# Attention scores as three fp32r products on split operands, and a scheduling priority for background work, in a decoder trunk on one core

## The chip, the cores and the metric

The kernel runs on one core of a Trainium2 chip. The metric is the device time in microseconds (us) of one execution. Five engines work side by side, each through its own instructions in order: TensorE (PE in the profile; its weight loads are listed apart as PEld), VectorE (DVE), ScalarE (ACT), GpSimd (POOL) and SyncE (SP), which issues most of the transfers. They wait for each other through semaphores.

## What is computed

One layer of a hybrid decoder trunk, for 256 positions of 2048 channels, in fp32:

```python
h = rms_norm(x, pre_g)
proj = h @ w_in        # a_u, a_v, a_g, b_x, b_g, x_q, x_g of 1024 columns each, gate_logits of 3 x 2048
y_a = spatial_gating(a_u, a_v, ...) * silu(a_g)      # layer norm of a_v over its 1024 channels first
y_b = s5_branch(b_x, ...) * silu(b_g)                # state-space scan, gelu, GLU
y_x = memory_cross_attention(x_q, rms_norm(mem, mem_g), xa_wk, xa_wv) * silu(x_g)
branch = einsum('bsnc,ncd->bsnd', stack([y_a, y_b, y_x]), w_branch)
merged = sum(sigmoid(gate_logits) * branch)
return x + rms_norm(merged @ w_out, post_g)

def memory_cross_attention(q, mem_n, w_k, w_v):      # 4 heads of 256 channels, 256 memory tokens
    k, v = mem_n @ w_k, mem_n @ w_v
    scores = einsum('bshd,bmhd->bhsm', qh, k) * 256 ** -0.5
    p = softmax(scores)
    return einsum('bhsm,bmhd->bshd', p, v)
```

## The kernel before

**Split weights.** Nearly every product is taken in the type fp32r, in three parts. `split` copies an operand to a high part in that type on ACT (L92) and subtracts it from the original on DVE, which gives the low part (L93, a buffer `hl` of 1024 columns of each; four such buffers rotate). A product is then high x high + high x low + low x high. A weight tile `raw` of 1 MB holds two such halves. A half of a block (`cm_block`, L174, L175, L177) or of a quarter (`tm_quarter`, L180 to L182) is what PE works through between two calls of `pump`; it is called a half-block below. The activations are split once and stay in SBUF.

**Stages.** The products run in this order: `w_bx`, the queries `w_xq`, the keys `wk`, the values `wv`, the gate `w_xg` of the attention branch, its gates and branch products (`merge`), then `w_av`, `w_ag`, `w_au` of the gating branch and its merge, `w_bg`, the gates, GLU and products of the S5 branch, and `w_out`. `cm_pairs` fills one PSUM pair (`acc`, two buffers in rotation) by four half-blocks and then empties it: ACT copies one part of it, and DVE adds the other (`fold_u`, L342 and L343, for queries and keys; `fold`, L230 and L231, elsewhere). PE can enter a pair only when the pair before the last one has been emptied, since it has the same bank.

**Background work.** Everything else is written as Python generators. Each call of `pump` lets every generator in the list `bg[2]` go on to its next `yield None`, and gives credit (0.47 to 1.5 a call, by the stage) to the S5 work in `bg[0]`; what a generator of `bg[2]` yields as a number is taken off that credit. In `bg[2]` are: `rms_row` (the norm of x, whose row `bc_x` is multiplied into `U` and the queries in eight steps, L330), `attn(h)` for four heads (scores L717, softmax L722 to L732, transposes `tp` L738), `attn_out(h)`, `layer_norm` (statistics L833, normalization by L371 and L374 on `H0`), and the transposes and gating steps later.

**Order.** PE's instructions stand in the order in which they are written. On DVE, ACT and the other engines a scheduler sets the order, by the place in the program and a priority; `split` of weights is written with a priority 250 places ahead (`AHEAD`), background work with none. The order is fixed when the kernel is built. The scores of a head are four products of plain fp32 operands of 128x256, each recorded as two entries in the profile (`x8`).

Of the kernel before, what the change touches and what calls it, by code (L numbers as in the profile page):

```python
# [10 lines left out]
F32R = mybir.dt.float32r  # L11
# [7 lines left out]
P = 128  # L19
# [12 lines left out]
PI2_3 = 2.0 * math.pi - PI2_1 - PI2_2  # L32
RND = 12582912.0
AHEAD = 250
BEHIND = 0
NWARM = 8
CM_OFF = 352 // 4
# [6 lines left out]
def trunk(ctx: ExitStack, tc: tile.TileContext, I, out):  # L44
    nc = tc.nc
    v, a, g, pe = nc.vector, nc.scalar, nc.gpsimd, nc.tensor
# [18 lines left out]
    def nm(s):  # L65
        n_[0] += 1
        return f"{s}_{n_[0]}"

    def slot(tag, shape, dt=F32):
        return big.tile(shape, dt, tag=tag, name=nm(tag))  # L70

    def small(shape, dt=F32):
        s = nm("sm")
        return const.tile(shape, dt, tag=s, name=s)
# [6 lines left out]
    def halves(off):  # L81
        t = hip.tile([P, 2 * 1024 + 128], F32R, tag="hl", name=nm("hl"))
        return t[:, off:off + 1024], t[:, off + 1024:off + 2048]

    def split(src, off=0):
        hi, lo = halves(off)
        with tc.high_priority(offset=AHEAD):
            split_to(hi, lo, src)
        return hi, lo

    def split_to(hi, lo, src):
        a.copy(out=hi, in_=src)  # L92
        v.tensor_tensor(out=lo, in0=src, in1=hi.bitcast(F32), op=ALU.subtract)  # L93
# [38 lines left out]
    def in_order2(z):  # L132
        return z.rearrange("p i (b c) -> p i c b", c=2)
# [29 lines left out]
    def norm_split(src, gv, dst, k0):  # L163
        for k in range(len(dst)):
            kk = k0 + k
            r = src[:, k * T:(k + 1) * T].rearrange("p (c b) -> p c b", c=2)
            hi, lo = dst[k].half(0), dst[k].half(1)
            a.activation(out=hi, in_=r, func=AF.Copy, scale=gv[:, kk:kk + 1])
            v.scalar_tensor_tensor(out=lo, in0=r, scalar=gv[:, kk:kk + 1],
                                   in1=hi.bitcast(F32), op0=ALU.mult, op1=ALU.subtract)  # L170
# [15 lines left out]
    def pump(credit):  # L186
        with tc.high_priority(offset=-BEHIND):
            pump_(credit)

    def pump_(credit):  # L190
        bg[1] += credit
        for gen in list(bg[2]):
            while True:
                c = next(gen, "end")
                if c == "end":
                    bg[2].remove(gen)
                    break
                if c is None:
                    break
                bg[1] -= c  # L200
        while bg[1] > 0:
            c = next(bg[0], "end")
            if c in (None, "end"):
                bg[1] = 0.0
                return
            bg[1] -= c
# [128 lines left out]
    def mem_half(hf):  # L335
        r = slot(f"M{hf}", [P, 2048])
        nc.sync.dma_start(out=r, in_=I["memT"][:, hf])
        with tc.high_priority(offset=AHEAD):
            norm_split(r, g_mem, mhl[hf * 8:hf * 8 + 8], hf * 8)
# [318 lines left out]
    qT = slot("X0", [P, 8, T])  # L658
# [16 lines left out]
    kT = slot("M0", [P, 8, T])  # L675
# [35 lines left out]
    def attn(h):  # L711
        for _ in range(4 * h):
            yield None
        sc = miscp.tile([P, 2, T], F32, tag="misc", name=nm("sc"))
        for qb in range(2):
            for c in range(2):
                pe.matmul(sc[:, qb, :], lhsT=qT[:, 2 * h + c, qb::2], rhs=kT[:, 2 * h + c, :],  # L717
                          start=c == 0, stop=c == 1)
        yield None
        nb = small([P, 2])  # L720
        sm = small([P, 2])
        v.tensor_reduce(out=nb, in_=sc, axis=AX.X, op=ALU.max)  # L722
        v.tensor_scalar(out=nb, in0=nb, scalar1=-1.0 / 16.0, scalar2=None, op0=ALU.mult)
        p = wk.tile([P, 2, T], F32, tag="w1", name=nm("p"))
        for qb in range(2):
            a.activation(out=p[:, qb, :], in_=sc[:, qb, :], func=AF.Exp, scale=1.0 / 16.0, bias=nb[:, qb:qb + 1],
                         accum_out=sm[:, qb:qb + 1])
        yield 0.7
        yield None
        v.reciprocal(out=sm, in_=sm)  # L730
        for qb in range(2):
            v.tensor_scalar(out=p[:, qb, :], in0=p[:, qb, :], scalar1=sm[:, qb:qb + 1], scalar2=None, op0=ALU.mult)  # L732
        yield 0.6
        yield None
        tp = miscp.tile([P, 2, T], F32, tag="misc", name=nm("tp"))
        for mb in range(2):
            for qb in range(2):
                pe.transpose(tp[:, mb, qb * P:(qb + 1) * P], p[:, qb, mb::2], ident)  # L738
        yield None
        a.copy(out=pT[:, h], in_=tp)  # L740

    def attn_out(h):
        for _ in range(h):
            yield None
        po = miscp.tile([P, 2, T], F32, tag="misc", name=nm("po"))
        for c in range(2):
            for mb in range(2):
                pe.matmul(po[:, c, :], lhsT=vv[:, mb, (2 * h + c) * P:(2 * h + c + 1) * P], rhs=pT[:, h, mb, :],  # L748
                          start=mb == 0, stop=mb == 1)
        yield None  # L750
        o = wk.tile([P, 2, T], F32, tag="w1", name=nm("o"))
        t = o.rearrange("p i (c b) -> p i c b", c=2)
        d = in_order2(sx[:, 2 * h:2 * h + 2, :])
        a.activation(out=t, in_=d, func=AF.Sigmoid)
        v.tensor_tensor(out=d, in0=po.rearrange("p i (c b) -> p i c b", c=2), in1=d, op=ALU.mult)
        yield 0.6
        v.tensor_tensor(out=t, in0=d, in1=t, op=ALU.mult)
        yield 0.6
        t = o
        d = yX[h // 2][:, 2 * (h % 2):2 * (h % 2) + 2]  # L760
        split_to(d[:, :, 0], d[:, :, 1], t)
        yield 1.2
# [3 lines left out]

    rate["cm"] = RT[2]
    bg[2].extend(attn(h) for h in range(4))
    cm_pairs(I["w_xg"], 8, xhl, evac_xg)
    bg[2].extend(attn_out(h) for h in range(4))  # L770

    mg = None
# [19 lines left out]
    def csl(c):  # L792
        return slice(c * 512, (c + 1) * 512)
# [116 lines left out]
    for bp in range(4):  # L910
# [9 lines left out]
        b = slice(2 * bp, 2 * bp + 2)  # L920
        v.tensor_tensor(out=t, in0=t, in1=u[:, b, :], op=ALU.mult)
        v.tensor_tensor(out=t, in0=t, in1=sb[:, b, :], op=ALU.mult)
        for i in range(2):
            d = yB[2 * bp + i]
# [25 lines left out]
    for c in range(4):  # L950
# [3 lines left out]
        for tb in range(2):  # L954
            d = sgB[tb][:, csl(c)]
# [68 lines left out]
    for tb in range(2):  # L1024
# [3 lines left out]
        c = slice(tb, tb + 1)  # L1028
# [107 lines left out]
```

## Time and profile before

| what | us |
|---|---|
| median of three runs (lowest, highest) | 913.08 (912.48, 913.41) |
| the profiled execution: time of its own | 913.93 |
| its span, from first to last instruction | 912.2 |
| TensorE busy | 899.3 (99%) |
| VectorE busy | 751.5 (82%) |
| ScalarE busy | 562.6 (62%) |

The mean granted clock of TensorE is 0.998 of full speed. Rows of a timeline give start, duration, engine, line, operation, tiles (written<-read) and form; "x3" stands for three instructions in a row, whose time is then that of all three. The duration of one instruction is longer than its pitch, since the next begins before it ends. Starts are counted from the span's start. A bracket gives idle time of the engine just before, and what ended it.

### The profile page before, as it was taken

How to read it: one execution, taken by the hardware profiler on the slowest of the kernel's cores; microseconds unless marked ns; L12 is line 12 of the kernel's file. 1: busy time of each engine (PE TensorE's matmuls, PEld its weight loads, DVE VectorE, ACT ScalarE, POOL GpSimd, SP SyncE). 2: the span in 40 equal slices, each digit the busy share in tenths (PEclk: the TensorE clock that was granted, in tenths of full speed). 3: DMA queues.
4: the chain of work that ended last, by engine and by line, in shares of the span. 5: the costliest groups of instructions: out<-in, count | busy, mean ns of one | idle time of the engine just before them, and what ended most of it. 6: DMA issues, size and time to landing. Idle time of an engine off the chain costs nothing.

```text
span 912.2 us, 12951 instructions
## 1 busy us (share of the span) xinstructions
PE 899.3 (99%) x4864; PEld 798.4 (88%) x4864; DVE 751.5 (82%) x1172; ACT 562.6 (62%) x962; POOL 49.8 (5%) x78
## 2 busy tenths in 40 slices
PE   8999999999999999999999999999999999999996
PEld 6999898889888888889989888889988889998896
DVE  6899967976779999899779998999889647876554
ACT  7585755855558677774456667767656546544452
POOL 1000000100001111110000010101000000000000
PEclk9999999999999999999999999999999999999999
DMA  9887665555455656665645656565655755557542
GB/s 337 312 311 294 226 231 194 202 193 191 154 205 176 242 187 227 231 212 207 231 167 186 221 203 212 190 213 203 231 190 194 258 195 203 211 185 277 194 175 93
DMA packets 32575, 195.30 MB, mean 214 GB/s; under 512 B 4224, under 2 KB 6528, under 8 KB 10752
## 3 DMA queue, kind: packets, MB, share of 16 engines
q1 hardware_dynamic: 28000, 186.08, 56.6%
q0 software_dynamic: 3936, 6.16, 3.1%
q10 hardware_dynamic: 576, 2.23, 0.6%
q8 instruction: 38, 0.62, 0.3%
q14 instruction: 25, 0.20, 0.1%
HBM read 190.39 MB, written 2.10 MB: 211 GB/s over the span
## 4 chain that ended last, share of the span: by engine, by line
PE 86%; DVE 9%; ACT 1%; DMA 1%; issue 1%; SPq 0%; DVEq 0%; ACTq 0%
PE acc L180 19%; PE acc L181 19%; PE acc L182 19%; PE acc L175 17%; PE acc L174 8%; DVE hl L93 4%; PE y L630 1%; ACT hl L92 1%; PE po L748 1%; DMA M<-memT 1%; DMA st<-start 1%; PE bu L568 1%; DVE q L374 1%; PE sc L717 1%; DVE tS L377 1%
## 5 line engine op out<-in xcount | busy, mean ns | idle before, releaser
L93 DVE TENSOR_TENSOR hl<-raw,hl 128x1024 fp32r<-128x1024 f32 x319 | 388.1, 1220 | 120.4 <-ACT hl L92 118.5
L92 ACT CAST hl<-raw 128x1024 fp32r<-128x1024 f32 x319 | 331.3, 1044 | 221.8 <-PE acc L182 139.1
L175 PE MATMUL acc<-x,hl 128*128 128x512 f32 x736 | 241.2, 382 | 0.0
L174 PE MATMUL acc<-x,hl 128*128 128x256 f32 x690 | 189.4, 274 | 2.6 <-DVE hl L93 2.6
L180 PE MATMUL acc<-hl,x 128*128 128x512 f32 x448 | 171.4, 383 | 0.0
L181 PE MATMUL acc<-hl,x 128*128 128x512 f32 x448 | 169.8, 379 | 0.0
L182 PE MATMUL acc<-hl,x 128*128 128x512 f32 x448 | 169.8, 379 | 0.0
L175 PEld LDWEIGHTS acc<-x,hl 128*128 128x128 f32 x736 | 136.8, 189 | 18.0 <-ACT hl L92 0.6
L174 PEld LDWEIGHTS acc<-x,hl 128*128 128x128 f32 x690 | 132.3, 192 | 4.5 <-DVE hl L93 3.2
L180 PEld LDWEIGHTS acc<-hl,x 128*128 128x128 f32 x448 | 84.7, 189 | 13.7 <-issue 2.5
L182 PEld LDWEIGHTS acc<-hl,x 128*128 128x128 f32 x448 | 84.7, 189 | 12.0
L181 PEld LDWEIGHTS acc<-hl,x 128*128 128x128 f32 x448 | 84.7, 189 | 11.3
L180 PE MATMUL acc<-hl,H 128*128 128x512 f32 (+1 forms) x224 | 83.6, 373 | 0.0
L181 PE MATMUL acc<-hl,H 128*128 128x512 f32 (+1 forms) x224 | 83.2, 372 | 0.0
L182 PE MATMUL acc<-hl,H 128*128 128x512 f32 (+1 forms) x224 | 83.2, 372 | 0.0
L175 PE MATMUL acc<-H,hl 128*128 128x512 f32 x192 | 62.6, 382 | 0.0
L539 POOL DMA_DIRECT2D B<-sb x30 | 25.4, 848 | 440.9 <-ACT B L534 409.4
L174 PE MATMUL acc<-H,hl 128*128 128x256 f32 x176 | 48.2, 274 | 0.2 <-DVE hl L93 0.2
L180 PEld LDWEIGHTS acc<-hl,H 128*128 128x128 f32 x224 | 42.4, 189 | 5.7 <-issue 0.4
L182 PEld LDWEIGHTS acc<-hl,H 128*128 128x128 f32 x224 | 42.4, 189 | 5.6
L181 PEld LDWEIGHTS acc<-hl,H 128*128 128x128 f32 x224 | 42.4, 189 | 5.3
L374 DVE TENSOR_TENSOR p<-bu,E 128x512 f32<-128x512 f32 x64 | 41.4, 684 | 1.7 <-PE bu L568 1.6
(256 smaller groups left out, 1217.7 us busy)
## 6 DMA issues: line engine op xcount, KB each, us to landing
raw<-w_gate SPq DMA_DIRECT2D x48, 1024.0 KB, 4.8
raw<-w_br SPq DMA_DIRECT2D x24, 1024.0 KB, 4.8
raw<-w_out SPq DMA_DIRECT2D x16, 1024.0 KB, 4.7
raw<-w_xq SPq DMA_DIRECT2D x8, 1024.0 KB, 5.2
raw<-wk SPq DMA_DIRECT2D x8, 1024.0 KB, 4.7
raw<-wv SPq DMA_DIRECT2D x8, 1024.0 KB, 4.9
raw<-w_xg SPq DMA_DIRECT2D x8, 1024.0 KB, 4.7
raw<-w_av SPq DMA_DIRECT2D x8, 1024.0 KB, 4.8
```

What stands on the lines that cost most here:

```text
L92: a.copy(out=hi, in_=src)
L93: v.tensor_tensor(out=lo, in0=src, in1=hi.bitcast(F32), op=ALU.subtract)
L174: pe.matmul(ps[:, 0:T], lhsT=wl, rhs=hl.moving(0), start=False, stop=False)
L175: pe.matmul(ps, lhsT=wh, rhs=hl.moving_both(), start=first, stop=last)
L180: pe.matmul(ps, lhsT=hl.stationary(0, tb), rhs=two(wh), start=first, stop=False)
L181: pe.matmul(ps, lhsT=hl.stationary(0, tb), rhs=two(wl), start=False, stop=False)
L182: pe.matmul(ps, lhsT=hl.stationary(1, tb), rhs=two(wh), start=False, stop=last)
L374: v.tensor_tensor(out=o, in0=i0, in1=i1, op=op)
L377: v.scalar_tensor_tensor(out=o, in0=i0, scalar=s, in1=i1, op0=o0, op1=o1)
L539: g.dma_start(out=B4[64:P].bitcast(F32), in_=rw[64:P], accum_op=ALU.add)
L568: pe.matmul(bu[:, ri, :], lhsT=B4[:, ri, :], rhs=two(U4), start=True, stop=True)
L630: pe.matmul(ps[32 * j:32 * j + 32, :], lhsT=cbt[:, cb * 4 + j, ri, :], rhs=ss[j][:, ri, :], start=ri == 0, stop=ri == 1, tile_position=(0, ...
```

## The change

Three things are written anew. The scores of a head are taken from split queries and keys: two `split_to` into a tile `qk` in the slot `H2` or `H3` (the split copies of the memory lie there until the values are done, and the attention output later), and then 12 fp32r products of 256 columns instead of four plain ones. The scores of a head come two pumps later than before, and so does `attn_out`. And all that the generators of `bg[2]` issue from `pump` gets a priority of 400 places (`URGENT`), which is ahead of the 250 of the weight splits.

```diff
+URGENT = 400
...
     def pump_(credit):
         bg[1] += credit
         for gen in list(bg[2]):
             while True:
-                c = next(gen, "end")
+                with tc.high_priority(offset=URGENT):
+                    c = next(gen, "end")
...
     def attn(h):
         for _ in range(4 * h):
             yield None
+        qk = slot(f"H{2 + h % 2}", [P, 2, 2, 2, 2, P], F32R)
+        for i, f in enumerate((qT, kT)):
+            d = f[:, 2 * h:2 * h + 2].rearrange("p k (b c) -> p k c b", c=2)
+            split_to(qk[:, i, :, :, 0], qk[:, i, :, :, 1], d)
+            yield 0.6
+        yield None
+        yield None
         sc = miscp.tile([P, 2, T], F32, tag="misc", name=nm("sc"))
         for qb in range(2):
             for c in range(2):
-                pe.matmul(sc[:, qb, :], lhsT=qT[:, 2 * h + c, qb::2], rhs=kT[:, 2 * h + c, :],
-                          start=c == 0, stop=c == 1)
+                q_, k_ = qk[:, 0, c], Pairs(qk[:, 1, c])
+                for i, (x_, y_) in enumerate(((0, 0), (0, 1), (1, 0))):
+                    pe.matmul(sc[:, qb, :], lhsT=q_[:, qb, x_], rhs=k_.moving(y_), start=c + i == 0, stop=c == 1 and i == 2)
...
     def attn_out(h):
-        for _ in range(h):
+        for _ in range(h + 2):
             yield None
```

Lines after `pump_` move by 2, those after the scores by 10: L93 is L94 in the new kernel, L330 is L332, L343 is L345.

**The order on DVE in the stage `wk`, around the fold of pair 0.** `acc_83` is that pair's PSUM bank, which pair 2 takes next; pair 2 begins with the split `hl_111`. Before:

```order
L93 TENSOR_TENSOR hl_106_1223<-raw_104_1198,hl_106_1223 128x1024
L343 TENSOR_TENSOR M0_81_1020<-acc_83_1022,M0_81_1020 128x512
L330 TENSOR_TENSOR U_1_129<-U_1_129,bc_x_1132 128x512 x3
L93 TENSOR_TENSOR hl_111_1253<-raw_110_1251,hl_111_1253 128x1024
L330 TENSOR_TENSOR U_1_129<-U_1_129,bc_x_1132 128x512
L330 TENSOR_TENSOR X0_39_551<-X0_39_551,bc_x_1132 128x512 x2
L93 TENSOR_TENSOR hl_112_1276<-raw_110_1251,hl_112_1276 128x1024
```

And in the new kernel:

```order
L94 TENSOR_TENSOR hl_106_1223<-raw_104_1198,hl_106_1223 128x1024
L332 TENSOR_TENSOR U_1_129<-U_1_129,bc_x_1132 128x512 x4
L94 TENSOR_TENSOR hl_111_1253<-raw_110_1251,hl_111_1253 128x1024
L332 TENSOR_TENSOR X0_39_551<-X0_39_551,bc_x_1132 128x512 x3
L94 TENSOR_TENSOR hl_112_1276<-raw_110_1251,hl_112_1276 128x1024
L332 TENSOR_TENSOR X0_39_551<-X0_39_551,bc_x_1132 128x512
L345 TENSOR_TENSOR M0_81_1020<-acc_83_1022,M0_81_1020 128x512
```

The fold of `acc_83` stood directly behind `hl_106`; now all eight multiplies by `bc_x` and two splits of pair 2 stand ahead of it. On ACT the cast of `uhl`, which reads `U`, has moved from behind to ahead of the cast of `hl_111`.

**The order on DVE in the stage `w_ag`, around the layer norm and the fold of pair 0.** Names carry other numbers in the two kernels: `acc_519` and `acc_513` are pair 0; `hl_537`, `hl_539`, `hl_543` of before and `hl_531`, `hl_533`, `hl_537` of the new kernel are the second, third and fourth split of pair 1, the next two those of pair 2, which takes pair 0's bank. Before:

```order
L93 TENSOR_TENSOR hl_537_4110<-raw_535_4087,hl_537_4110 128x1024
L371 TENSOR_SCALAR H0_451_3562<-H0_451_3562,sm_523_3996,sm_526_4021 128x512 x2
L374 TENSOR_TENSOR H0_451_3562<-H0_451_3562,X0_453_3567 128x512 x2
L93 TENSOR_TENSOR hl_539_4132<-raw_538_4130,hl_539_4132 128x1024
L374 TENSOR_TENSOR H0_451_3562<-H0_451_3562,X0_453_3567 128x512 x2
L93 TENSOR_TENSOR hl_543_4158<-raw_538_4130,hl_543_4158 128x1024
L231 TENSOR_TENSOR f_532_4079<-acc_519_3973,f_532_4079 128x512
```

In the new kernel, from the last of the eight tiny rows that now stand behind the second split:

```order
L107 TENSOR_TENSOR sm_539_4194<-sm_539_4194,sm_540_4195 128x1
L373 TENSOR_SCALAR H0_450_3591<-H0_450_3591,sm_517_4012,sm_520_4037 128x512 x2
L376 TENSOR_TENSOR H0_450_3591<-H0_450_3591,X0_452_3596 128x512 x4
L108 SCALAR_TENSOR_TENSOR sm_538_4193<-sm_539_4194,sm_538_4193 128x1
L94 TENSOR_TENSOR hl_533_4148<-raw_532_4146,hl_533_4148 128x1024
L373 TENSOR_SCALAR H0_450_3591<-H0_450_3591,sm_535_4168,sm_538_4193 128x512 x2
L376 TENSOR_TENSOR H0_450_3591<-H0_450_3591,X0_452_3596 128x512 x4
L94 TENSOR_TENSOR hl_537_4174<-raw_532_4146,hl_537_4174 128x1024
L94 TENSOR_TENSOR hl_545_4218<-raw_544_4216,hl_545_4218 128x1024
L94 TENSOR_TENSOR hl_546_4239<-raw_544_4216,hl_546_4239 128x1024
L233 TENSOR_TENSOR f_526_4095<-acc_513_3989,f_526_4095 128x512
```

Both chunks' normalizations stand whole ahead of the third and the fourth split, where the second chunk's was spread over the fold and the splits that follow; the fold has moved behind the two first splits of pair 2.

**The order on DVE at head 0's softmax, in the stage `w_xg`.** `sm` and `p` belong to the softmax, `E`, `s`, `p1` and `p2` to the S5 work, `H2` to the split queries and keys of head 2. Before:

```order
L93 TENSOR_TENSOR hl_217_2012<-raw_216_2010,hl_217_2012 128x1024
L722 TENSOR_REDUCE sm_207_1950<-sc_205_1926 128x2
L377 SCALAR_TENSOR_TENSOR E_260_2362<-E_260_2362,pwr_547,t_289_2558 128x2x64
L723 TENSOR_SCALAR sm_207_1950<-sm_207_1950 128x2
L374 TENSOR_TENSOR s_290_2563<-p2_262_2365,E_188_1855 128x512
L374 TENSOR_TENSOR s_290_2563<-p1_261_2364,s_290_2563 128x512
L93 TENSOR_TENSOR hl_219_2037<-raw_216_2010,hl_219_2037 128x1024
L730 RECIPROCAL sm_208_1951<-sm_208_1951 128x2
L732 TENSOR_SCALAR p_209_1954<-p_209_1954,sm_208_1951 128x256 x2
```

And in the new kernel:

```order
L94 TENSOR_TENSOR hl_222_2070<-raw_221_2068,hl_222_2070 128x1024
L732 TENSOR_REDUCE sm_211_2003<-sc_209_1971 128x2
L94 TENSOR_TENSOR H2_232_2158<-X0_39_551,H2_232_2158 128x4x128
L733 TENSOR_SCALAR sm_211_2003<-sm_211_2003 128x2
L94 TENSOR_TENSOR H2_232_2158<-M0_81_1020,H2_232_2158 128x4x128
L376 TENSOR_TENSOR s_298_2662<-p1_287_2602,s_298_2662 128x512
L740 RECIPROCAL sm_212_2004<-sm_212_2004 128x2
L379 SCALAR_TENSOR_TENSOR E_308_2731<-E_308_2731,pwr_547,t_311_2737 128x2x32
L742 TENSOR_SCALAR p_213_2007<-p_213_2007,sm_212_2004 128x256 x2
L94 TENSOR_TENSOR hl_224_2103<-raw_221_2068,hl_224_2103 128x1024
```

The weight split that stood between the maximum and the normalization now stands behind both, and two splits for head 2 have come between them.

## The prediction

> **What bounds the kernel now.** I read the page's engine line and its chain first, then the list of what PE waited for, then a table of busy time by stretches of 38 us (columns: stretch, then busy us of PE, PEld, DVE, ACT and POOL, granted clock, DMA).
>
> ```profile
> PE 899.3 (99%) x4864; PEld 798.4 (88%) x4864; DVE 751.5 (82%) x1172; ACT 562.6 (62%) x962; POOL 49.8 (5%) x78
> ...
> PE 86%; DVE 9%; ACT 1%; DMA 1%; issue 1%; SPq 0%; DVEq 0%; ACTq 0%
> ```
>
> ```profile
> PE acc L174 <- DVE hl L93: 2.7, 3, 1.5
> ...
> PE tp L738 <- DVE p L732: 0.8, 1, 0.8
> ```
>
> ```profile
> 190.00:228.00 38.00, 37.24 (x223) 34.33 (x223) 24.12 (x38) 20.70 (x34) 0.00 (x0) 1.00 0.54 198
> ```
>
> TensorE is busy in 899.3 of 912.2 us and carries 86% of the chain. A microsecond of PE work taken out is a microsecond of the run, and a microsecond in which PE stands is one too, since PE has no idle time in which to catch up. The wait list says how little there is to win by faster background work: behind the start, PE waits for one background product, the transposes `tp`, for 0.8 us. So I cost three things: PE work removed, that wait, and any new wait. A new wait can come from VectorE (DVE), which runs in its written order and has the weight splits, the folds that free PSUM banks, and all background work in one queue.
>
> **Part 1: the score products.** Rows of PE in order of time; then the chain's row for a later head.
>
> ```profile
> 180.02 0.27 PE L174 MATMUL acc<-x,hl 128*128 128x256 f32 x1
> 180.13 0.38 PE L175 MATMUL acc<-x,hl 128*128 128x512 f32 x1
> 180.35 1.89 PE L717 MATMUL sc<-M,X 128*128 128x256 f32 x8
> 181.89 0.46 PE L174 MATMUL acc<-x,hl 128*128 128x256 f32 x1
> ```
>
> ```profile
> 194.28 1.73 PE sc L717 x8
> ```
>
> A head's scores cost 1.73 us of PE on the chain. The new form issues 12 fp32r products of 256 columns; such a product is L174's, and it takes 0.11 us from start to start (180.02 to 180.13). 12 x 0.11 is 1.31 us, so 0.42 us less per head, and four heads give **-1.7 us**. Bounds: 0 if the first product of each head has to wait for its stationary load, -2.0 if the 12 run without any join; -1.7 lies on measured pitches and is taken.
>
> The splits that feed them are two per head, each one ACT cast and one DVE subtraction of 128x512, so 8 of each. ACT: 8 x 0.57 (row 106.44 below, the nearest shape) is 4.6 us; DVE: 8 x 0.60 (the L330 rows below, 1.81 us for three) is 4.8 us. The quoted stretch from 190 has 24.12 us of DVE and 20.70 us of ACT in 38, so there they lie beside PE. They cost nothing there, provided the scores come two pumps (two half-blocks of PE) later, as the order has them. They also use 4.8 us of the credit that paces the S5 work, so that work comes later: by up to four half-blocks in PE's order, 10.5 us. The last `y` products started at 723.1, and the GLU stage, which needs them, begins behind the gate sigmoids of 755.71:
>
> ```profile
> L630 PE MATMUL y<-s,cb x128: 379/379/403, 267.8 to 723.1; 128*32 128x256 f32 x128
> ```
>
> ```profile
> 755.71 1.26 ACT L903 ACTIVATE H<-acc,sm 128x512 f32<-128x512 f32 x2
> ```
>
> Some 20 us of cover remain there: nothing. Bounds 0 to +1, if in one of the dense S5 stretches a weight split slips.
>
> **Part 2: the `tp` wait.** PE rows of head 0 and of head 1:
>
> ```profile
> 189.72 0.38 PE L175 MATMUL acc<-x,hl 128*128 128x512 f32 x1
> 190.86 0.80 PE L738 MATMUL tp<-ident,p 128*128 128x128 f32 x4 [0.76 <-DVE p L732]
> 191.41 0.46 PE L175 MATMUL acc<-x,hl 128*128 128x512 f32 x1
> ...
> 203.70 0.63 PE L738 MATMUL tp<-ident,p 128*128 128x128 f32 x4
> 204.09 0.46 PE L175 MATMUL acc<-x,hl 128*128 128x512 f32 x1
> ```
>
> A 512-column product has a pitch of 0.22 us (180.13 to 180.35), so head 0's transposes could have started at 189.94; they started at 190.86 and took 0.55 us where head 1's took 0.39. That is 1.1 us. In the new order head 0's softmax stands ahead of a weight split, but the splits of queries and keys of three heads stand in front of it or between its steps, and PE asks for it two pumps later. Adding the row durations up along DVE's new order, I get the transposes' input about 0.3 us after PE wants it: **-0.8 us**, bounds -1.1 (no wait left) and 0 (the same wait at a new place).
>
> **Part 3: what the priority puts behind.** In the order, 63 PSUM pairs are emptied; 61 folds stand against the splits as before. Two have moved behind two splits of the block that reuses their bank.
>
> First place: the `wk` stage, pair 0 (`acc_83`, whose bank pair 2 takes). DVE, then ACT, then PE, of before:
>
> ```profile
> 107.16 1.22 DVE L93 TENSOR_TENSOR hl<-raw,hl 128x1024 fp32r<-128x1024 f32 x1
> 108.29 0.69 DVE L343 TENSOR_TENSOR M<-acc,M 128x512 f32<-128x512 f32 x1
> 108.89 1.88 DVE L330 TENSOR_TENSOR U<-U,bc_x 128x512 f32<-128x512 f32 x3
> 110.70 1.22 DVE L93 TENSOR_TENSOR hl<-raw,hl 128x1024 fp32r<-128x1024 f32 x1
> 111.83 0.68 DVE L330 TENSOR_TENSOR U<-U,bc_x 128x512 f32<-128x512 f32 x1
> 112.43 1.28 DVE L330 TENSOR_TENSOR X<-X,bc_x 128x512 f32<-128x512 f32 x2
> 113.64 1.21 DVE L93 TENSOR_TENSOR hl<-raw,hl 128x1024 fp32r<-128x1024 f32 x1
> ```
>
> ```profile
> 106.44 0.57 ACT L342 COPY M<-acc 128x512 f32<-128x512 f32 x1
> ...
> 107.23 1.04 ACT L92 CAST hl<-raw 128x1024 fp32r<-128x1024 f32 x1
> 109.61 0.87 ACT L92 CAST uhl<-U 128x256 fp32r<-128x256 f32 x1 [1.34 <-DVE U L330]
> 110.51 0.82 ACT L541 CAST U<-uhl 32x256 fp32r<-32x256 f32 x2
> ```
>
> ```profile
> 113.77 0.60 PE L175 MATMUL acc<-H,hl 128*128 128x512 f32 x2
> ```
>
> The fold stood at 108.29; PE enters pair 2 with the second of the two products from 113.77, at 113.99. In the new order four U multiplies follow the split of 107.16: 108.29 + 4 x 0.60 = 110.70. The cast for the next split now stands behind ACT's `uhl`, which waits for the first U multiply: from 109.0 for 0.87, then the cast to 110.9. The split runs 110.95 to 112.08, three X multiplies to 113.89, a split to 115.02, one X to 115.62, and only then the fold, to 116.31. PE resumes near 116.35: **+2.3 us**. Bounds +1.8 (the cast is not in the way) and +2.8.
>
> Second place: `w_ag`, pair 0, whose bank pair 2 takes; here the layer norm (L371, L374 on `H0`) is drawn together ahead of two splits. DVE and PE of before:
>
> ```profile
> 417.82 1.22 DVE L93 TENSOR_TENSOR hl<-raw,hl 128x1024 fp32r<-128x1024 f32 x1
> 418.96 1.00 DVE L371 TENSOR_SCALAR H<-H,sm,sm 128x512 f32<-128x512 f32 x2
> 419.87 1.29 DVE L374 TENSOR_TENSOR H<-H,X 128x512 f32<-128x512 f32 x2
> 421.08 1.22 DVE L93 TENSOR_TENSOR hl<-raw,hl 128x1024 fp32r<-128x1024 f32 x1
> 422.21 1.29 DVE L374 TENSOR_TENSOR H<-H,X 128x512 f32<-128x512 f32 x2
> 423.42 1.22 DVE L93 TENSOR_TENSOR hl<-raw,hl 128x1024 fp32r<-128x1024 f32 x1
> 424.55 0.69 DVE L231 TENSOR_TENSOR f<-acc,f 128x512 f32<-128x512 f32 x1
> 425.15 0.15 DVE L107 SCALAR_TENSOR_TENSOR sm<-sm,sm 128x1 f32<-128x1 f32 x1
> ```
>
> ```profile
> 408.68 0.38 PE L175 MATMUL acc<-x,hl 128*128 128x512 f32 x1
> ...
> 418.94 0.60 PE L175 MATMUL acc<-x,hl 128*128 128x512 f32 x2
> ```
>
> PE enters pair 0 at 408.68 and pair 1 at 419.16, so a half-block takes 2.62 us. The three splits shown are the second, third and fourth of pair 1, wanted at 421.78, 424.40 and 427.02; they end at 418.96, 422.21 and 424.55. The fold ends at 425.15, and pair 2 wants its bank at 429.64. The slack is 2.8, 2.2, 2.5 and 4.5 us. In the new order, counted from the second split, there stand: ahead of the third, eight tiny rows (0.1 us each) and one chunk's whole normalization (0.91 + 4 x 0.60 = 3.3), which is 1.9 us more than before; ahead of the fourth, the other chunk's 3.3 in place of 1.2, so 4.0 more in all; ahead of the fold two further splits, 6.3 more. What is left is 0.3, -1.5 and -1.8: PE waits 1.5 us for the fourth split and a little more for the bank, **+1.8 us**. This takes the second split's own slack as unchanged. S5 work comes later, and DVE could be up to 1.2 us earlier or later there, which gives +0.6 and +3.0.
>
> **Sum.** -1.7 - 0.8 + 2.3 + 1.8 = +1.6 us. The profiled execution took 913.93 us (a span of 912.2 and 1.7 outside), 0.85 over the median of the runs. It would become 915.5; the median 913.08 becomes **914.7**.
>
> **A rule weighed.** Stalls of 2 us touch the granted clock only if it reacts to them. The stretch from 190 has a PE gap of 0.9 us and a clock of 1.00. The Trainium skill (TensorE: Matmul & The Clock Gate, "HAM oscillation — how this bites in real kernels") has PE fall to half rate after an idle gap of about 3.4 us. By that rule the sum stands, since both stalls lie under it, and the trace agrees as far as its 0.9 us goes.
>
> **Rivals.**
> - *Only the first stall.* DVE reaches `w_ag` early, as it has less S5 work behind it, and the second place fits into its slack; it needs 1.8 us there. -1.7 - 0.8 + 2.3 = -0.2: 912.9. For it: the S5 work is late by 4.8 us of credit. Against it: the slacks of 2.2 to 2.8 us show a DVE that is not waiting for anything. Chance 0.25.
> - *Neither stall, faster.* PE finds both banks free, as the moved folds end before 113.99 and 429.64. It decides only if DVE gets to the first fold 2.3 us sooner than by its rows, which needs two multiplies and a split not to be in front; the order has them there. -2.5: 910.6. Chance 0.13.
> - *More stalls.* The second stall at its upper bound (+1.2), or splits late where S5 work and scores collide (+1), or the `tp` wait unchanged (+0.8). Two of these together: 916.6 to 917. Chance 0.12.
> - *The clock falls behind a stall.* If PE then ran at half rate for as long as it had stood, each stall costs half as much again: +2.0, 916.7. Chance 0.05. By the Trainium skill's page named above (TensorE: Matmul & The Clock Gate, the same section), a stall would have to be longer than either.
>
> **Numbers.** Both stalls (0.45) gives 914.7, within 913.3 and 916.2. A difference of 0.2%, 1.8 us, is about what a measurement here tells from none: slower is above 914.9, faster below 911.25. Of the 0.45, 0.22 lies above and 0.23 below 914.9. Slower: 0.22 + 0.12 + 0.05 = 0.39. Same: 0.23 + 0.23 of the first rival and 0.01 of the second = 0.47. Faster: 0.12 + 0.02 = 0.14. The range leaves out most of the "neither" case and the far end of "more": 911.0 to 916.9.
>
> **What would show it.** Score products of about 1.3 us per head; a PE gap of about 2.3 us in `wk` behind the fold of the first pair, with the fold after two splits; one near 430 us behind a split or fold of `w_ag`, 1 to 3 us; `tp` gaps under 0.5 us. The forecast is wrong if the first gap is absent, if `w_ag` shows none, or if gaps appear between 200 and 720 us elsewhere.

## The result: 919.4 us, slower, and the profile after

| | before | changed |
|---|---|---|
| median of five runs, us | 913.08 (912.48 to 913.99) | 919.38 (917.57 to 919.72) |
| the profiled execution: own time, span, us | 913.93, 912.2 | 918.3, 916.6 |

The changed kernel takes 1.0061 times as long [1.005, 1.0073]: 6.3 us more, above the forecast of 914.7 and outside its range. L93 of before is L94 now, L343 is L345, L330 is L332, L371 and L374 are L373 and L376, L231 is L233, the scores are L728 and `tp` is L748.

The engine line and the chain from the page of the changed kernel:

```profile
PE 899.8 (98%) x4880; PEld 797.8 (87%) x4880; DVE 757.9 (83%) x1180; ACT 567.5 (62%) x970; POOL 49.1 (5%) x78
...
PE 78%; DVE 14%; ACT 3%; issue 2%; DMA 1%; SPq 0%; DVEq 0%; ACTq 0%
```

PE has as many busy microseconds as before in a span that is 4.4 us longer: PE stands longer. DVE's share of the chain went from 9% to 14%. Its list of what PE waited for says where (us in total, times, longest):

```profile
PE acc L175 <- DVE hl L94: 3.5, 4, 1.8
PE acc L176 <- DVE M L345: 2.2, 1, 2.2
...
PE tp L748 <- DVE p L742: 0.9, 1, 0.9
PE acc L178 <- DVE hl L94: 0.8, 1, 0.8
```

Two waits are new, that for a fold (`M`, L345) and that of L178, the first low-weight product of a block, for a split. Of the first row's 3.5 us, 1.8 are new, in `w_ag`; the rest lies at the start of the run, where the kernel before waited 2.7. The `tp` wait, forecast to go, is still there.

**The scores.** The chain's row for a later head:

```profile
201.48 1.34 PE sc L728 x12
```

1.34 us a head where 1.73 stood: 0.39 less, for four heads 1.56 us.

**The `wk` gap.** DVE around the first fold of the keys, and PE there:

```profile
106.98 1.22 DVE L94 TENSOR_TENSOR hl<-raw,hl 128x1024 fp32r<-128x1024 f32 x1
108.12 2.49 DVE L332 TENSOR_TENSOR U<-U,bc_x 128x512 f32<-128x512 f32 x4
110.63 1.23 DVE L94 TENSOR_TENSOR hl<-raw,hl 128x1024 fp32r<-128x1024 f32 x1
111.77 1.89 DVE L332 TENSOR_TENSOR X<-X,bc_x 128x512 f32<-128x512 f32 x3
113.58 1.22 DVE L94 TENSOR_TENSOR hl<-raw,hl 128x1024 fp32r<-128x1024 f32 x1
114.72 0.68 DVE L332 TENSOR_TENSOR X<-X,bc_x 128x512 f32<-128x512 f32 x1
115.32 0.68 DVE L345 TENSOR_TENSOR M<-acc,M 128x512 f32<-128x512 f32 x1
```

```profile
113.58 0.38 PE L176 MATMUL acc<-H,hl 128*128 128x512 f32 x1
116.15 0.45 PE L176 MATMUL acc<-H,hl 128*128 128x512 f32 x1 [2.19 <-DVE M L345]
```

Between the norm's eight multiplies stand the weight splits, and behind the last multiply the fold, at 115.32 where it stood at 108.29. PE resumes when it is done. From start to start the two products are 2.57 us apart instead of 0.22: 2.35 us lost.

**The `w_ag` gaps.** DVE and PE in the first two pairs of `w_ag`:

```profile
419.55 1.22 DVE L94 TENSOR_TENSOR hl<-raw,hl 128x1024 fp32r<-128x1024 f32 x1
...
421.45 1.00 DVE L373 TENSOR_SCALAR H<-H,sm,sm 128x512 f32<-128x512 f32 x2
422.37 2.49 DVE L376 TENSOR_TENSOR H<-H,X 128x512 f32<-128x512 f32 x4
...
424.85 1.22 DVE L94 TENSOR_TENSOR hl<-raw,hl 128x1024 fp32r<-128x1024 f32 x1
425.98 1.00 DVE L373 TENSOR_SCALAR H<-H,sm,sm 128x512 f32<-128x512 f32 x2
426.90 2.49 DVE L376 TENSOR_TENSOR H<-H,X 128x512 f32<-128x512 f32 x4
429.30 3.49 DVE L94 TENSOR_TENSOR hl<-raw,hl 128x1024 fp32r<-128x1024 f32 x3
```

```profile
422.36 0.27 PE L175 MATMUL acc<-x,hl 128*128 128x256 f32 x1
...
426.12 0.38 PE L178 MATMUL acc<-x,hl 128*128 128x256 f32 x1 [0.76 <-DVE hl L94]
...
430.58 0.38 PE L175 MATMUL acc<-x,hl 128*128 128x256 f32 x1 [1.78 <-DVE hl L94]
```

At 422.36 PE wants the second split of pair 1 and finds it done. Each chunk of the layer norm lies whole in front of one of the next two splits, as forecast, and PE waits behind both: 0.93 and 1.95 us from start to start over the usual pitch, and 0.32 more for the bank at 433.8, together 3.2 us.

**The `tp` wait.** DVE during head 0's softmax, and the transposes:

```profile
194.62 0.68 DVE L732 TENSOR_REDUCE sm<-sc 128x2 f32<-128x512 f32 x1
195.22 0.77 DVE L94 TENSOR_TENSOR H<-X,H 128x512 fp32r<-128x512 f32 x1
195.91 0.16 DVE L733 TENSOR_SCALAR sm<-sm 128x2 f32<-128x2 f32 x1
195.98 0.80 DVE L94 TENSOR_TENSOR H<-M,H 128x512 fp32r<-128x512 f32 x1
...
197.56 0.62 DVE L742 TENSOR_SCALAR p<-p,sm 128x256 f32<-128x256 f32 x2
```

```profile
198.06 0.80 PE L748 MATMUL tp<-ident,p 128*128 128x128 f32 x4 [0.87 <-DVE p L742]
```

The subtractions of the query and key splits (`H<-X,H` and `H<-M,H`) stand in the middle of the softmax, 1.4 us of them from start to start; behind them comes 0.8 us of S5 work. The transposes could have started at 197.02 and started at 198.06: 1.04 us, where it was 0.92 before.

**The clock.** The medians hold something that this profile does not show. A second profile of the same kernel (below) fell on an execution of 919.82 us. It has the same gaps, but behind the `wk` gap PE runs at half rate. The trace's records of the clock give the half rate from 116.14 to 119.56. PE's busy time in the 3.41 us ahead of 116.14, from there on, and behind (stretch, length, busy, products, then granted clock and DMA):

```profile
112.73:116.14 3.41, 1.22 (x8) 1.00 0.12 22
116.14:119.56 3.42, 3.42 (x12) 0.50 0.71 285
119.56:122.97 3.41, 3.41 (x22) 1.00 0.38 120
```

Stretches of the same length in the 918.3 us execution:

```profile
112.21:115.63 3.42, 1.75 (x11) 1.00 0.01 2
115.63:119.04 3.41, 2.89 (x18) 1.00 0.88 308
```

Busy time does not show the half rate; the count of products does, 12 in 3.42 busy microseconds against 18 in 2.89, and so does the granted clock, 0.50 against 1.00. In 3.4 us of half rate PE falls 1.7 us behind. The ten executions of this kernel lie in two groups, 916.8 to 918.3 and 919.4 to 920.0, with a mean granted clock of 0.997 to 0.999 in the first and 0.995 to 0.997 in the second.

### The profile page after: what moved, and what is told of

Its sections match the earlier page's. It is cut to its first block, busy times and chain, and to the rows that moved or that the text cites. A ratio compares the mean times of both kernels' runs of the same rounds, so it can differ in the third digit from the quotient of the medians.

```text
span 916.6 us, 12996 instructions
## 1 busy us (share of the span) xinstructions
PE 899.8 (98%) x4880; PEld 797.8 (87%) x4880; DVE 757.9 (83%) x1180; ACT 567.5 (62%) x970; POOL 49.1 (5%) x78
## 4 chain that ended last, share of the span: by engine, by line
PE 78%; DVE 14%; ACT 3%; issue 2%; DMA 1%; SPq 0%; DVEq 0%; ACTq 0%
PE acc L181 18%; PE acc L182 17%; PE acc L183 17%; PE acc L176 14%; PE acc L175 7%; DVE hl L94 6%; ACT hl L93 1%; PE y L632 1%; DVE p L376 1%; DMA M<-mem 1%; DVE s L376 1%; PE po L758 1%; DVE H L170 1%; DMA st<-start 1%; PE bu L570 1%
## 5 line engine op out<-in xcount | busy, mean ns | idle before, releaser
L94 DVE TENSOR_TENSOR hl<-raw,hl 128x1024 fp32r<-128x1024 f32 x319 | 387.9, 1221 | 117.5 <-ACT hl L93 115.5
L93 ACT CAST hl<-raw 128x1024 fp32r<-128x1024 f32 x319 | 331.2, 1045 | 210.5 <-PE acc L183 125.0
L376 DVE TENSOR_TENSOR p<-bu,E 128x512 f32<-128x512 f32 x64 | 41.7, 682 | 1.1 <-PE bu L570 0.9
```

Of the source, the lines that this page charges most:

```text
L376: v.tensor_tensor(out=o, in0=i0, in1=i1, op=op)
```

## The experiments

Ratios are to runs of the kernel before on the same chip. Lines of the variants are numbered one or more higher than in the changed kernel, up to L95 for the splits' L94.

**1. The scores without the priority**

```diff
-URGENT = 400
+URGENT = 0
```

> The new scores with the priority of the background work set to 0 (URGENT = 0). Theory (the priority's two moved folds cost the time, the scores gain 1.6 us): no PE gap in wk and none at w_ag; 1.34 us of PE per head instead of 1.73, -1.6. In this order head 0's normalization stands behind a weight split and a fold, about 1.9 us later than in the changed kernel, so the tp gap is about 3 us instead of 1.1: +1.9. Sum +0.3: 913.4 (912.4 to 914.4). Rival (the later scores and the later S5 work cost the time, whatever the priority): 916 or more, with gaps at w_ag as in the changed kernel.

Measured: 921.46 us, ratio 1.0096 [1.0082, 1.0109]. PE's waits, and the granted clock behind two of them:

```profile
PE tp L748 <- DVE p L742: 6.7, 3, 3.0
```

```profile
198.00:200.00 2.00, 1.39 (x6) 0.53 0.85 360
216.00:218.00 2.00, 2.00 (x9) 0.50 0.72 287
```

The `wk` and `w_ag` gaps are absent, so these are the priority's doing. But the new scores without it are the worst version: heads 0 and 1 each make PE stand for some 3 us ahead of their transposes, and each time the clock halves (1.5 and 1.7 us lost). The forecast of 913.4 counted head 0 alone, and no clock. Whether later transposes would do instead of the priority was not tried.

**2. The priority without the new scores.** `attn` and `attn_out` are those of before; `URGENT` is 400.

```diff
-        qk = slot(f"H{2 + h % 2}", [P, 2, 2, 2, 2, P], F32R)
...
+                pe.matmul(sc[:, qb, :], lhsT=qT[:, 2 * h + c, qb::2], rhs=kT[:, 2 * h + c, :],
+                          start=c == 0, stop=c == 1)
...
-        for _ in range(h + 2):
+        for _ in range(h):
```

> The kernel before with the priority alone (scores as before). Theory: the wk gap of 2.3 us is there as in the changed kernel; the tp gap of 1.1 us is gone, since the softmax stands ahead of a split there; at w_ag a gap of 1.8 us, as worked out from the rows of the kernel before, because the S5 work is not late here: +2.3 - 1.1 + 1.8 = +3.0: 916.1 (915 to 917.2). Rival 1 (the w_ag gap has nothing to do with late S5 work): 3.2 us at w_ag, 917.5. Rival 2 (the scores cost the time): 913, no gaps.

Measured: 917.47 us (916.64 to 918.37), 1.005 [1.0037, 1.0062]:

```profile
PE acc L175 <- DVE hl L94: 2.2, 3, 1.6
PE acc L176 <- DVE M L345: 2.2, 1, 2.2
PE acc L178 <- DVE hl L94: 1.4, 1, 1.4
```

The `tp` wait is gone and the `wk` gap is the same. The `w_ag` gaps are 2.1 us where the changed kernel has 3.2, so 1.1 us of those come with the new scores. They are not quite the same gaps: here the chunks of the layer norm stand ahead of the second and the third split of pair 1, and no longer of the third and the fourth. The median is above the forecast and its range. The profiled execution, of 916.73 us, has a whole clock behind the `wk` gap; the three at 917.5 to 918.4 have a mean clock of 0.995 to 0.996, the other two one of 0.997 and 0.999, so a half clock in those three is likely, but none of them was profiled.

**3. The norms without the priority.** The two norm generators are drawn without it; attention and the rest keep it.

```diff
+CALM = ("rms_row", "layer_norm")
...
-                with tc.high_priority(offset=URGENT):
+                with tc.high_priority(offset=0 if gen.__name__ in CALM else URGENT):
```

> The changed kernel, with the two norm generators (rms_row and layer_norm) left without the priority; the attention generators keep it. The folds of both places stand again where they stood before. Theory: no gap in wk, none at w_ag; scores -1.6, the tp gap stays near 1.1 us: 911.5 (910.5 to 912.5). Rival (the priority of the attention work or the late S5 work costs time too): 914 or more.

Measured: 911.71 us, 0.9987 [0.9979, 0.9996], with all `wk` and `w_ag` gaps gone and this left:

```profile
PE tp L749 <- DVE p L743: 1.0, 1, 1.0
```

The loss came from the priority of two generators that PE does not wait for in those places. Against experiment 1 (921.46) it also gives the value of the priority for attention and the other work that keeps it, once the scores are new: 9.8 us, about 3 of them clock. With the old scores and no priority PE waits 0.8 us there.

**4. The changed kernel again,** with no edit.

> The changed kernel once more, for its spread and for a second profiled execution. Theory: the gaps follow from a fixed order, so wk 2.3 us and w_ag about 3.2 us again, time 918 to 920. Rival (the time between 917.6 and 919.7 comes from gaps that vary with the arrival of transfers): the gaps differ by 0.5 us or more between the two profiles, or a new one appears.

Measured: 917.06 us (916.77 to 919.98), 1.0052 [1.0039, 1.0066], and the profile with the half clock shown above.

**5. A ladder of gaps.** The kernel of experiment 3 with 26 gaps made in PE's stream: between two added products stand POOL memsets of a set length, in a mixed order of lengths, which the second product waits for.

```diff
+    def gap():
...
+        pe.matmul(ps, lhsT=gz[:, 0:P], rhs=gz, start=True, stop=True)
+        while n > 0:
+            g.memset(gz[:, 0:min(n, 512)], 0.0)
+            n -= 512
+        pe.matmul(ps, lhsT=gz[:, 0:P], rhs=gz, start=True, stop=True)
```

> The changed kernel without the priority of the norms, and with 26 gaps made on PE in the tm stages: a small product, POOL memsets of a set length behind it, and a product that waits for them; the set lengths go from about 0.8 to 3.4 us in steps of some 0.2, in a mixed order, each two or three times. Theory (a PE gap of 2 to 3 us can halve the granted clock for some 3.3 us, as seen behind gaps of 2.2, 2.8 and 3.0 us): no slow stretch behind gaps under about 1.5 us, one behind each gap over 2.6 us, and at 1.8 to 2.4 us one in some; each costs about 1.6 us beyond the gap. Rival (the slow stretches came from something else, such as the transfers that run on during the gap): no relation to the length. By the Trainium skill (TensorE: Matmul & The Clock Gate, HAM oscillation — how this bites in real kernels) nothing should happen under about 3.4 us.

Measured: 1018.44 us (one run), and gaps somewhat longer than set. Behind the eleven of 0.73 to 2.22 us the clock stays whole. Of the fifteen of 2.39 to 5.96 us, fourteen have a half clock behind them. It lasts 2.6 to 5.7 us from the gap's end and costs half of that, 1.3 to 2.8 us, in no order of the gap's length: 5.7 us behind a gap of 3.21, 2.6 behind one of 2.89. The one exception has 3.19 us. The 4 us behind gaps of 2.22, 3.19 and 3.19 us:

```profile
356.40:360.40 4.00, 4.00 (x18) 1.00 0.75 244
421.90:425.90 4.00, 4.00 (x11) 0.59 0.82 295
448.60:452.60 4.00, 4.00 (x18) 1.00 0.91 274
```

**6. The folds ahead of everything.** Both kinds of fold get priority 500, above the background's 400.

```diff
+FOLDS = 500
...
+        with tc.high_priority(offset=FOLDS):
+            a.copy(out=d, in_=ps[..., T:2 * T])
+            v.tensor_tensor(out=d, in0=ps[..., 0:T], in1=d, op=ALU.add)
```

> The changed kernel with the folds and their copies at a priority of 500, above that of the background work. Theory: the wk gap is a wait for the PSUM bank alone and goes; at w_ag the weight splits still stand behind the layer norm, so the gaps of 0.9 and 1.9 us stay and only the last 0.3 us, behind the fold, goes. Time about 915 (calm_norms 911.7 + 2.9). Rival (the w_ag gaps are the bank's too): both places without gaps, 912.

Measured: 915.55 us (one run).

```profile
PE acc L176 <- DVE hl L95: 3.1, 3, 1.8
...
PE acc L179 <- DVE hl L95: 1.4, 1, 1.4
PE tp L751 <- ACT hl L94: 1.4, 1, 1.4
```

The bank's wait in `wk` disappears; those in `w_ag` stay, 1.59 and 1.95 us over the pitch, since there PE waits for a split and not for a fold. The `tp` wait grew to 1.4 us, behind a cast on ACT; why was not followed up.

**7. The transposes of head 0 one pump later,** on the kernel of experiment 3.

```diff
-        for _ in range(4 * h):
+        for _ in range(4 * h + (h > 0)):
...
+        if h == 0:
+            yield None
...
-        for _ in range(h + 2):
+        for _ in range(h + 3):
```

> calm_norms with head 0's transposes one pump later, the further heads and the attention outputs one pump later too. Theory: the 1.1 us gap at tp goes and nothing takes its place: calm_norms 911.7 - 1.1 = 910.6 (909.9 to 911.3), faster than both kernels. Rival (another background product is late then): a gap at tp or po of 0.5 us or more, 911.3 or above.

Measured: 910.53 us (909.99 to 911.01), 0.9976 [0.9967, 0.9985]. The `tp` wait is gone from its list, and 1.2 us with it (1.0 by the ratios). This version is ahead of both kernels.

**8. Only the layer norm without the priority:** the `wk` gap alone.

```diff
+CALM = ("layer_norm",)
```

> The changed kernel with only the layer norm left without the priority; rms_row keeps it. Theory: the wk gap of 2.35 us alone on top of calm_norms: 914.1 in executions whose clock holds behind the gap and 915.7 in those where it halves for 3.3 us; so the runs fall into two groups some 1.6 us apart. No gap at w_ag. Rival (the spread of the changed kernel comes from w_ag): one group, within 1 us, at 914.

Measured: 915.28 us, 1.0027 [1.0015, 1.0039], spread over 2.9 us: three executions at 913.4 to 914.9, with a mean clock of 0.997 to 0.999, and three at 915.7 to 916.3, with 0.996 to 0.997. That fits two groups and not one within 1 us, but six executions do not show a cut between them. The profile fell on 914.14 and shows the gap with a whole clock behind it:

```profile
PE acc L177 <- DVE M L346: 2.2, 1, 2.2
```

**9 and 10. The same gap shorter, and longer,** on the kernel of experiment 8. For 9, two multiplies by the norm's row are left out (the scaling of the last two query blocks, so their values are unscaled). For 10, a spare DVE copy stands ahead of the fold.

```diff
-            for i in range(4):
+            for i in range(3 if m == "q" else 4):
```

```diff
-    def fold_u(d, ps):
+    def fold_u(d, ps, spare=None):
...
+        if spare is not None:
+            with tc.high_priority(offset=URGENT):
+                v.tensor_scalar(out=spare, in0=d, scalar1=1.0, scalar2=None, op0=ALU.mult)
```

> calm_ln with the wk gap made shorter: the norm multiply of the last two query blocks is left out, which stood ahead of the fold (0.6 us). Gap about 1.75 us. Theory (the two groups of times come from the clock halving behind a gap of 2.2 us in some executions, and the ladder shows none at 2.06 us or less): one group, 911.7 + 1.75 = 913.4 (912.7 to 914.2), no slow stretch. Rival (the two groups have another cause): again two groups 1.6 us apart or more.

> calm_ln with the wk gap made longer: a spare DVE copy of 128x512 ahead of the fold (some 0.5 us). Gap about 2.8 us. Theory: the clock halves behind it in nearly every execution, as behind 13 of 14 gaps over 2.39 us in the ladder: one group at 911.7 + 2.8 + 1.7 = 916.2 (915.4 to 917). Rival: two groups again, at 914.5 and 916.2.

Measured: 913.73 us (913.0 to 914.28, eleven executions), 1.0006 [0.9997, 1.0015], and 916.45 us (915.73 to 916.53, five), 1.0037 [1.0024, 1.0049]. The waits of the shorter one, then of the longer one, and the longer one's clock behind it:

```profile
PE acc L177 <- DVE M L346: 1.6, 1, 1.6
```

```profile
PE acc L177 <- DVE M L349: 2.6, 1, 2.6
```

```profile
116.00:118.00 2.00, 2.00 (x9) 0.50 0.77 320
```

PE stands 0.98 us longer in the second (2.73 us over the pitch against 1.75), and the time is 2.7 us longer; the halved clock accounts for the other 1.7 (1.66 in the two profiles, by when the same products start). Neither has two groups: the gap of 2.2 us lies where the clock sometimes halves, 1.6 below it and 2.6 above it.

**11. Only the norm of x without the priority:** the `w_ag` gaps alone.

```diff
+CALM = ("rms_row",)
```

> The changed kernel with only rms_row left without the priority; the layer norm keeps it. Theory: the wk gap is gone, the w_ag gaps of 0.9, 1.9 and 0.3 us stay, each under 2.1 us and so without a slow stretch: one group at 911.7 + 3.2 = 914.9 (914.2 to 915.7). Rival (the w_ag gaps depend on the wk gap, which shifts PE against DVE): under 2 us at w_ag, 913.5.

Measured: 915.03 us (914.46 to 915.8, eleven executions in one group), 1.0023 [1.0014, 1.0032].

```profile
PE acc L176 <- DVE hl L95: 3.2, 4, 1.8
PE acc L179 <- DVE hl L95: 0.8, 1, 0.8
```

3.3 us more than experiment 3, as the gaps' 3.2 say, with no halved clock behind them: PE is idle for at most 1.8 us in each. So the `w_ag` gaps do not hang on the `wk` gap.

## Why the prediction was wrong

- **Scores:** right. 1.56 us less, forecast 1.7; of the 0.42 us a head, 0.39 came.
- **First stall (`wk`):** right in place, cause and size: 2.35 us, forecast 2.3, with the DVE rows in the forecast order. The fold began at 115.32, where the rows added up gave 115.62.
- **Second stall (`w_ag`):** right in mechanism, mis-sized: 3.2 us, forecast 1.8. The step that failed is "this takes the second split's own slack as unchanged". The split ended at 420.7 and was wanted at 422.36, a slack of 1.65 us, not 2.8. That is 1.15 less, nearly the 1.2 that the prediction kept as its bound, and the whole of it was due: slacks of 0.3, -1.5 and -1.8 us less 1.15 are -0.85, -2.65 and -2.95, and PE lost 0.93, 2.88 and 3.20 us in all by these three points. The later S5 work fits as the cause: its two rows `s` (L376, 413.01 to 414.34) stand ahead of the last split before the layer norm, where neither the kernel before nor experiment 2 has them, and experiment 2, without the new scores, has gaps of 2.1 us. No run moved these rows alone. The work that the prediction found covered at its end, where the last `y` product started at 740.4 and the gate sigmoids at 760.05, was not covered on the way there.
- **The `tp` wait:** wrong; 0.8 us was booked as a gain and none came. The step was the sum of DVE rows that put the transposes' input 0.3 us after PE wants it. It came about 1.04 after. The prediction gives this sum without its rows, so which of them was short stays open. The profile shows 1.4 us of query and key splits and 0.8 us of S5 work between the softmax's steps; experiment 7 shows that one pump more removes the wait.
- **The clock:** wrong, in "by that rule the sum stands" and in the chance of 0.05. The rule of the Trainium skill (TensorE: Matmul & The Clock Gate, "HAM oscillation — how this bites in real kernels"), no PE-idle gaps beyond about 3.4 us, does not hold here. The rate halves behind most gaps from 2.39 us and, in some executions, behind one of 2.2; the measurement decides. The rival's price went wrong too: not half of the stall again, but about 1.7 us at once, and behind the first stall only. The trace of before could show nothing on this, since its longest gap quoted was 0.9 us; a rule with no row near its threshold should have had more than 0.05.

The own times of the profiled executions close the account at a whole clock: 915.5 was forecast and 918.3 came. Of these 2.8 us, 1.4 are `w_ag`, 0.8 `tp`, 0.2 the scores and the first stall, and about 0.4 arise between 462 and 755 us, which I have not placed; experiment 3 loses 0.3 us there too and experiment 2 nothing, so they come with the new scores. The median adds the clock: it lies in the upper group of executions. Built up from experiment 3, 911.7 + 2.35 + 3.2 is 917.3, which is already above the range's 916.9, and, with 1.7 for the clock, 919.0; the two groups are at 916.8 to 918.3 and 919.4 to 920.0. That the groups are the halved clock is shown for one execution of this kernel and supported, by the size, the mean clocks and the absence of groups, by experiments 9 to 11; the other executions were not profiled.

So the change holds three things with different signs: new scores that in this place need the priority (experiment 1), the priority for attention, worth 9.8 us with them, and the same priority for two norms, which costs 5.6 us of stalls and, often, 1.7 of clock.

## What to carry to other kernels

Give a priority to the work that PE waits for, by name, and not to all background work: whatever else takes it stands in front of weight splits and of the folds that free PSUM banks. Price a DVE queue by the slack at each split, and take work that arrives later into that slack. When a change makes PE stand for more than 2 us, a half clock can come on top, some 1.7 us in most cases here; look at the count of products behind the gap, since busy time hides it.

## What the runs showed of the hardware that was not expected

- PE's granted clock halved behind 14 of 15 made gaps of 2.39 to 5.96 us, behind gaps of 2.75 and 3.0 us in experiment 1 and behind the one of 2.57 us in experiment 10. The half clock cost 1.3 to 2.8 us, mostly 1.7. Behind gaps up to 2.06 us it never came; at 2.2 us it came in one of four profiles of kernels with the `wk` gap, and not in the one gap of that length in the ladder.
- Near that length one kernel has two groups of times, 918.3 us and below and 919.4 us and above, with the same instruction order and the same gaps. The traces point to what decides. In each of the thirteen the clock's records change only at points a whole number of 3.413 us apart, on a grid that lies differently from execution to execution; ahead of the run's end a half clock lasts one such stretch, twice in the ladder two. Behind every full-clock stretch with 2.06 us or more of idle PE the clock is halved, and behind none with 1.99 us or less; at 2.04 us there is one of each (the ends of products, and so the idle times, are modelled). In the execution of 919.82 us the whole `wk` gap lies in one stretch (busy 1.22 of 3.41, above); in that of 918.3 us the grid cuts it at 115.63. The two ladder gaps of 3.19 us, the one with the half clock and then the exception, which is cut at 446.55:

```profile
419.24:422.66 3.42, 0.76 (x3) 1.00 0.27 36
...
443.14:446.55 3.41, 2.20 (x12) 1.00 0.69 243
446.55:449.96 3.41, 1.43 (x6) 1.00 0.58 135
```

This was read from the traces afterwards, and no run was made to test it. By it a gap of 2.57 us could escape too if it were cut near its middle; the five executions of experiment 10 show no such case.
